# Mixers' tiles in pairs of 8 KB, the normed rows in two tiles of 16 KB, and experts' weights loaded in packets of 8 and 16 KB

## The chip, the cores and the metric

The kernel runs on one core of a Trainium2 chip. The metric is the device time of one execution in microseconds; the time of the kernel before is the median of three runs, 1653.99 us (1653.51 to 1654.05). The profile was taken from one execution of it. PE is TensorE, DVE VectorE, ACT ScalarE, POOL GpSimd and SP SyncE. SP computes nothing here: it issues nearly all of the loads.

## What the kernel computes

The reference is an encoder trunk of two layers on 512 rows of 1024 (float32). What matters of it is this:

```
for l in range(DEPTH):                       # 2
    hn = rmsnorm(x, norm_mix_w[l])
    proj = hn @ w_in[l]                      # the four mixers' columns
    mix = concat([hyena, mamba2, attention, hgrn2])
    x = x + mix @ w_out[l]
    x = x + expert_choice_moe(rmsnorm(x, norm_ffn_w[l]), router_w[l], moe_w_gate[l], moe_w_up[l], moe_w_down[l])
return rmsnorm(x, final_norm_w)

def expert_choice_moe(x, w_router, w_gate, w_up, w_down):   # 16 experts, 64 rows each
    gate, idx = top_k(softmax(x @ w_router), cap)
    xe = x[idx]
    hdn = silu(xe @ w_gate) * (xe @ w_up)    # 1024 x 1024 each
    ye = (hdn @ w_down) * gate
    return rows of ye added at idx
```

Each expert has three matrices of 4 MB, so a layer's experts have 192 MB (201 million bytes) of weights, and each is used once.

## The kernel before

A layer has two stages. In the first, the rows of x are normed and turned (`norm_T`, tiles `hT`), multiplied with the columns of `w_in`, and worked on by four mixers, whose instructions are woven together by a planner. In the second, the router's ranks pick 64 rows for each expert, and the experts follow one another on PE in the order in which they are written: up(e), the turned rows of a later expert, gate(e+1), the hidden columns, down(e); after every second expert `combine` adds the weighted rows to x (`eoT`, `eot` and `ec`: a matmul that turns the pair's ranks, a comparison on DVE, and the matmuls that place the rows).

Weights come in by `pieces` (L1371 to L1398). A matrix of an expert is 8 rows of 512 KB, each 128 partitions x 4 KB; in main memory four rows of one partition lie side by side, so that a DMA of n rows moves n x 4 KB in one run per partition. A piece goes into a slot of a pool, whose tag is taken from the list `ring`. The pools are shared with the mixers: before, H has 12 slots of 4 KB (4 hold x, 8 the turned normed rows, of which weights use 7), N 9 and B 13 of 4 KB, W 2 of 8 KB and S 3 of 8.25 KB. A slot of W or S takes two rows by one DMA, unless k is 3 or 7; then the second half is kept in `spare` and is the next row's. All else takes one row. A tile can go to a slot when the last reader of the tile that had it is done, and for a tile that was loaded in two DMAs that is the reader of its later half.

All of these DMAs stand in one queue, SP's. Its order is fixed when the program is built, by a scheduler that follows the order of the text except where it expects a slot to come free late; then it may put a DMA behind others. At run time SP takes them one after the other: one that waits holds all behind it. Eight semaphores (DMAHW0 to DMAHW7 below) are shared by them in turn. The order of PE, DVE and ACT is fixed in the same way.

The names below: `we` is a tile of weights, `eg`, `eu` and `ey` are the sums of gate, up and down, `exT` and `ehT` their turned inputs, `eh` the hidden rows, `eY` the weighted rows. The number behind a name is that of the tile.

Of the kernel before, what the change touches and what calls it, by code (L numbers as in the profile page):

```python
# [11 lines left out]
F32R = mybir.dt.float32r  # L12
# [82 lines left out]
NN, NB, NW, NS, NG, NEP, NPA = 9, 13, 2, 3, 9, 2, 3  # L95
# [15 lines left out]
def encoder(ctx: ExitStack, tc: tile.TileContext, d, out, dbg=None, stages=None, nlayers=NL):  # L111
# [6 lines left out]
    slots = {"H": (12, 4096), "N": (NN, 4096), "B": (NB, 4096), "W": (NW, 8192), "S": (NS, 8448),  # L118
             "G": (NG, 2048), "E": (NEP, 2048)}
# [82 lines left out]
    X = [tl("H", [D], "x") for _ in range(4)]  # L202
# [124 lines left out]
    def norm_T(l, rows, side=iter(())):  # L327

        hl = [[tl("H", [2, L], "hT", F32R) for _ in range(4)] for _ in range(2)]

        def scaled(q):
            xs = [tl("B", [D], "xn") for _ in range(2)]
# [16 lines left out]
        def turned(q, xs):  # L349
            for k in range(8):  # L350
# [7 lines left out]
                h, o = (hl[i][k // 2][:, k % 2, q * 256:(q + 1) * 256] for i in range(2))  # L358
# [14 lines left out]
        return ([hl[0][k // 2][:, k % 2] for k in range(8)], [hl[1][k // 2][:, k % 2] for k in range(8)])  # L373
# [79 lines left out]
    def mix_tile(m):  # L453
        MIX[m] = (tl("B", [2, L], "mxh", F32R), tl("B", [2, L], "mxl", F32R))
# [25 lines left out]
    def filter_consts():  # L480
        dec = tl("B", [4, 256], "dec")
        SY.dma_start(dec, d["c_decay"].rearrange("(t p) c -> p t c", p=P))
        kt = [tl("B", [4, 256], "kt") for _ in range(2)]
        for i in range(2):
            SY.dma_start(kt[i], d["c_kdft"][i].rearrange("(t p) f -> p t f", p=P))
        return dec, kt
# [48 lines left out]
    def filter_spec(spec, h, w3, fb, dec, kt, scratch=None):  # L535

        ab = [tl("B", [2, 2, 256], "fab") for _ in range(2)]
# [43 lines left out]
    def hyena_proj(l, hT, cols, st):  # L581
        raw1 = w_raw(l, HY0 + 256, 256)
        raw2 = w_raw(l, HY0 + 512, 256)
        uT = tl("N", [4, 256], "uT")
# [16 lines left out]
        x0 = tl("N", [2, L], "hx0")  # L601
# [8 lines left out]
    def hyena(l, st, spec):  # L610
        uT, x0 = st
        ct, it = tl("B", [2, 4, P], "dft"), tl("B", [2, 4, P], "idft")
# [3 lines left out]
        xs = [tl("B", [2, 2, 256], "hX") for _ in range(2)]  # L616
# [35 lines left out]
        zs = [tl("B", [2, 2, 256], "hz") for _ in range(2)]  # L652
# [990 lines left out]
```

## Time and profile before

| | |
|---|---|
| median of 3 runs | 1653.99 us (1653.51 to 1654.05) |
| profiled execution | 1657.14 us, span 1655.4 us |
| mean granted TensorE clock | 0.971 |
| PE busy | 1531.7 us, 93% of the span |
| DVE, ACT, POOL busy | 802.6, 396.1, 213.8 us |
| moved by DMA | 468.54 MB, 283 GB/s over the span |
| chain that ended last | PE 63%, DMA 25%, DVE 6% |
| experts' matmuls, gate, up, down (L1404) | 230.7, 237.9, 233.1 us |
| experts' DMAs of 512 KB, and of 1024 KB | 632, and 68 |

The span is what the profiler saw from the first to the last instruction. Busy time is the share in which an engine worked at all; the chain is followed back from the last instruction, at each step to what released it.

### The profile page before, as it was taken

What the parts mean: (1) busy time and instruction counts of PE and PEld (TensorE: products, weight loads), DVE (VectorE), ACT (ScalarE), POOL (GpSimd) and SP (SyncE); (2) the same over time, 40 slices, a digit from 0 to 9 for tenths busy, and PEclk for the clock granted to TensorE, in tenths of its full rate; (3) what the DMA queues carried; (4) which work ended last, traced back from release to release, by engine and by line L of the source; (5) the groups of instructions that cost most, each with busy time, mean ns of one, the idle gap of its engine ahead of it and who ended that gap; (6) DMA issues with size and microseconds to landing.
All of it is one profiled execution on the core that took longest, in us unless ns stands there. A gap on an engine that the chain in (4) does not pass through costs nothing.

```text
span 1655.4 us, 22757 instructions
## 1 busy us (share of the span) xinstructions
PE 1531.7 (93%) x8899; PEld 880.2 (53%) x8899; DVE 802.6 (48%) x1727; ACT 396.1 (24%) x805; POOL 213.8 (13%) x214
## 2 busy tenths in 40 slices
PE   6989998989999998989979999999899999998985
PEld 5778787763433432334368788787434433332332
DVE  6777677573333331432256767856533333332323
ACT  4344333431000000001162435243200001000012
POOL 3232133000000000000033232310000000000001
PEclk9989899999999999999989889999899999999998
DMA  5411223679999999999932202167799999999996
GB/s 169 127 51 36 68 77 141 239 288 341 421 420 421 421 420 399 421 420 420 419 95 82 72 27 77 54 233 266 262 407 418 420 422 420 421 420 421 420 420 247
DMA packets 153773, 468.54 MB, mean 283 GB/s; under 512 B 20440, under 2 KB 56696, under 8 KB 144962
## 3 DMA queue, kind: packets, MB, share of 16 engines
q1 hardware_dynamic: 145030, 455.10, 70.3%
q0 software_dynamic: 2240, 7.34, 1.1%
q10 hardware_dynamic: 6396, 4.65, 0.8%
q8 instruction: 70, 1.15, 0.3%
q14 instruction: 37, 0.30, 0.0%
HBM read 460.60 MB, written 6.44 MB: 282 GB/s over the span
## 4 chain that ended last, share of the span: by engine, by line
PE 63%; DMA 25%; DVE 6%; ACT 3%; issue 2%; POOL 1%; ACTq 0%; SPq 0%; DVEq 0%; POOLq 0%
PE eg L1404 9%; DMA we<-in_moe_w_up_dram 9%; DMA we<-in_moe_w_down_dram 9%; PE eu L1404 8%; PE ey L1404 7%; DMA we<-in_moe_w_gate_dram 5%; PE pcm L395 3%; PE pcm L396 3%; PE pcm L397 3%; PE ec L1475 2%; PE po L1222 2%; PE po L1223 2%; PE po L1224 2%; PE ptm L418 2%; PE ptm L417 2%
## 5 line engine op out<-in xcount | busy, mean ns | idle before, releaser
L1404 PE MATMUL eu<-we,exT 128*64 128x512 f32 x1024 | 237.9, 598 | 17.2 <-DMA we<-in_moe_w_up_dram 14.9
L1404 PE MATMUL ey<-we,ehT 128*64 128x512 f32 x1024 | 233.1, 600 | 17.3 <-ACT ehT L1440 11.2
L1404 PE MATMUL eg<-we,exT 128*64 128x512 f32 x1024 | 230.7, 598 | 10.4 <-DMA we<-in_moe_w_gate_dram 6.4
L1404 PEld LDWEIGHTS eu<-we,exT 128*64 128x64 f32 x1024 | 67.7, 136 | 181.6 <-issue 91.9
L1303 DVE SCALAR_TENSOR_TENSOR ra<-er,ra,tie 128x512 bf16<-128x512 f32 x128 | 95.9, 749 | 128.6 <-PE er L1311 125.7
L1404 PEld LDWEIGHTS ey<-we,ehT 128*64 128x64 f32 x1024 | 70.2, 137 | 155.5 <-issue 102.1
L1404 PEld LDWEIGHTS eg<-we,exT 128*64 128x64 f32 x1024 | 69.2, 136 | 149.6 <-issue 111.5
L1457 DVE SCALAR_TENSOR_TENSOR eY<-ey,erg,eY 64x512 fp32r<-64x512 f32 x64 | 48.0, 750 | 189.2 <-ACT eY L1456 189.1
L1425 ACT ACTIVATE eh<-eg 128x512 f32<-128x512 f32 x32 | 19.1, 598 | 498.6 <-PE eg L1404 498.6
L397 PE MATMUL pcm<-hT,whl 128*128 128x512 f32 x320 | 128.9, 403 | 3.5 <-DVE whl L381 3.5
L1476 DVE TENSOR_TENSOR x<-x,ec 128x512 f32<-128x512 f32 x128 | 81.0, 691 | 102.6 <-PE ec L1475 102.5
L396 PE MATMUL pcm<-hT,whl 128*128 128x512 f32 x320 | 130.2, 407 | 0.0
L395 PE MATMUL pcm<-hT,whl 128*128 128x512 f32 x320 | 129.9, 406 | 0.0
L1348 POOL DMA_INDIRECT exe<-xd,erow x28 | 27.8, 994 | 787.0 <-DVE erg L1329 660.1
L1456 ACT ACTIVATE eY<-ey,erg 64x512 fp32r<-64x512 f32 x64 | 43.7, 683 | 268.3 <-PE ey L1404 243.9
L1432 DVE TENSOR_TENSOR eh<-eh,eu 128x512 f32<-128x512 f32 x32 | 22.0, 687 | 153.9 <-PE eu L1404 153.9
L417 PE MATMUL ptm<-wtm,hT 128*128 128x256 f32 (+1 forms) x256 | 76.1, 298 | 1.7 <-DVE aqs L926 1.7
L1475 PE MATMUL ec<-eY,eot 128*128 128x512 f32 x256 | 67.3, 405 | 10.2 <-DVE erow L1346 6.4
L418 PE MATMUL ptm<-wtm,hT 128*128 128x256 f32 (+1 forms) x256 | 74.2, 291 | 1.3 <-DVE wtm L381 1.3
L380 POOL TENSOR_SCALAR whl<-wraw 128x1024 fp32r<-128x1024 f32 x40 | 46.9, 1173 | 220.1 <-PE pcm L397 127.7
L419 PE MATMUL ptm<-wtm,hT 128*128 128x256 f32 (+1 forms) x256 | 72.8, 288 | 0.0
L397 PEld LDWEIGHTS pcm<-hT,whl 128*128 128x128 f32 x320 | 62.3, 195 | 18.2 <-DVE whl L381 3.9
(394 smaller groups left out, 2374.8 us busy)
## 6 DMA issues: line engine op xcount, KB each, us to landing
we<-in_moe_w_gate_dram SPq DMA_DIRECT2D x218, 512.0 KB
we<-in_moe_w_up_dram SPq DMA_DIRECT2D x208, 512.0 KB
we<-in_moe_w_down_dram SPq DMA_DIRECT2D x206, 512.0 KB
wraw<-in_w_in_dram SPq DMA_DIRECT2D x27, 1024.0 KB
we<-in_moe_w_down_dram SPq DMA_DIRECT2D x25, 1024.0 KB
we<-in_moe_w_up_dram SPq DMA_DIRECT2D x24, 1024.0 KB
we<-in_moe_w_gate_dram SPq DMA_DIRECT2D x19, 1024.0 KB
wo<-in_w_out_dram SPq DMA_DIRECT2D x8, 1024.0 KB
```

The costliest lines, as they stand in the source:

```text
L380: G.tensor_scalar(dst_hi, raw, 1.0, 0.0, op0=ALU.mult, op1=ALU.add)
L395: T.matmul(ps, w[:, 0, k, :], H[k], start=(k == 0), stop=False)
L396: T.matmul(ps, w[:, 0, k, :], Lo[k], start=False, stop=False)
L397: T.matmul(ps, w[:, 1, k, :], H[k], start=False, stop=(k == 7))
L417: T.matmul(dst, h, w[:, 0, k % 4], start=(k == 0), stop=False)
L418: T.matmul(dst, h, w[:, 1, k % 4], start=False, stop=False)
L419: T.matmul(dst, g, w[:, 0, k % 4], start=False, stop=(k == 7))
L1303: V.scalar_tensor_tensor(g, pr, ra[:, c, e, 0:1], tie[:, 384 - c * P:896 - c * P], op0=ALU.subtract, op1=ALU.is_gt, accum_out=k)
L1404: T.matmul(ps[f][64 * f:64 * f + 64], xT[:, j, h], qs[4 * h + j][:, f * 512:(f + 1) * 512], start=(h == 0 and j == 0), stop=(h == 1 and j ...
L1457: V.scalar_tensor_tensor(lo, src, w[c, 0:1], hi.bitcast(F32), op0=ALU.mult, op1=ALU.subtract)
L1475: T.matmul(ps, ot[:, t * P:(t + 1) * P], Y[i][q][n], start=(q == 0), stop=(q == 1))
L1476: V.tensor_add(xrow(t)[:, c], xrow(t)[:, c], ps)
```

## The change

The pools are cut anew, with the same bytes in all. x has a pool of its own (X, 4 x 4 KB). The turned normed rows lie in two tiles of 16 KB (H). N has 4 and B 6 slots of 8 KB; V and C are single slots of 4 KB. The mixers' tiles that had one slot of 4 KB each are put together in twos into one tile of 8 KB and used as its halves (`MIX`, `xn`, `kt`, `fab`, `hX`, `hz`, `gqk`, `gU` with `gw`, and so on); what is left single goes to V (`gv`, `av`, `ra`) and to C (`oh`, `dec`, `mpack`). In `pieces`, a DMA takes as many rows as the tile has and as are left of the four that lie side by side. What a tile has over is kept in `spare`, and is used only for a place where the number of rows left has the same parity; so a rest can stay until a later matrix. A layer's 384 rows are then 190 DMAs in layer 0 and 193 in layer 1 where they were 351 and 349: 14 and 20 of one row, 167 and 164 of two, 9 of four. The matmuls and the engines' operations are the same in number.

```diff
-NN, NB, NW, NS, NG, NEP, NPA = 9, 13, 2, 3, 9, 2, 3
+NN, NB, NW, NS, NG, NEP, NPA = 4, 6, 2, 3, 9, 2, 3
...
-    slots = {"H": (12, 4096), "N": (NN, 4096), "B": (NB, 4096), "W": (NW, 8192), "S": (NS, 8448),
-             "G": (NG, 2048), "E": (NEP, 2048)}
+    slots = {"X": (4, 4096), "H": (2, 16384), "N": (NN, 8192), "V": (1, 4096), "B": (NB, 8192), "C": (1, 4096),
+             "W": (NW, 8192), "S": (NS, 8448), "G": (NG, 2048), "E": (NEP, 2048)}
...
-        hl = [[tl("H", [2, L], "hT", F32R) for _ in range(4)] for _ in range(2)]
+        hl = [tl("H", [8, L], "hT", F32R) for _ in range(2)]
...
-            xs = [tl("B", [D], "xn") for _ in range(2)]
+            xp = tl("B", [2, D], "xn")
+            xs = [xp[:, i] for i in range(2)]
...
-        MIX[m] = (tl("B", [2, L], "mxh", F32R), tl("B", [2, L], "mxl", F32R))
+        hl = tl("B", [2, 2, L], "mix", F32R)
+        MIX[m] = hl[:, 0], hl[:, 1]
...
-        dec = tl("B", [4, 256], "dec")
+        dec = tl("C", [4, 256], "dec")
...
-        pack = tl("B", [576], "mpack")
+        pack = tl("C", [576], "mpack")
...
-        v = tl("N", [4, 256], "av")
+        v = tl("V", [4, 256], "av")
...
-        v = tl("N", [4, 256], "gv")
+        v = tl("V", [4, 256], "gv")
...
-            qk, qi, bes = yield from hgrn_decay(l, i, q, f, lb, keep)
-            R = [tl("B", [64, 16], "gR") for _ in range(2)]
+            qi = qis[:, i]
+            qk, bes = yield from hgrn_decay(l, i, q, f, lb, keep, qi)
+            R = tl("B", [2, 64, 16], "gR")
+            R = [R[:, e] for e in range(2)]
...
-        rt = tl("H", [D], "ra")
+        rt = tl("V", [D], "ra")
...
-    FIRST = ["N"] * 2 + ["B"]
-    EARLY = ["N"] * 3 + ["B"] * 6 + ["N"] * (NN - 5) + ["B"] * (NB - 7)
+    FIRST = ["N", "C"]
+    EARLY = ["N"] + ["B"] * 3 + ["N"] * (NN - 2) + ["B"] * (NB - 3)
     LATE = ["W"] * NW + ["S"] * NS
     ring = []
 
+
     SIDE_AT = 9
-    RESTED = (["N"] * 2 + ["B"] * 6 + ["N"] * (NN - 4) + ["H"] * 7 + LATE) * 6
+    RESTED = (["N"] + ["B"] * (NB - 3) + ["N"] * (NN - 2) + ["H"] * 2 + LATE) * 6
 
     def pieces(l, view):
 
@@ -1379,20 +1396,20 @@
             rows = d["moe_w_" + m][l, e].rearrange("(h p j) f -> h p j f", h=2, p=P)
             v = view[e, m] = []
             while len(v) < 8:
+
                 k = len(v)
-                n = 1
-                if spare:
-                    t = spare.pop()
+                left = 4 - k % 4
+                t = next((t for t in spare if t.shape[1] % 2 == left % 2), None)
+                if t is not None:
+                    spare.remove(t)
                 else:
                     if not ring:
-                        ring.extend(FIRST + EARLY + ["H"] * 7 + LATE)
+                        ring.extend(FIRST + EARLY + ["H"] * 2 + LATE)
                     tag = ring.pop(0)
                     t = tl(tag, [slots[tag][1] // 4096, D], "we")
-                    if t.shape[1] == 2:
-                        if k % 4 != 3:
-                            n = 2
-                        else:
-                            spare.append(t[:, 1:])
+                n = min(t.shape[1], left)
+                if n < t.shape[1]:
+                    spare.append(t[:, n:])
                 SY.dma_start(t[:, :n], rows[k // 4][:, k % 4:k % 4 + n, :])
...
-        ring[:] = LATE + FIRST + ["H"] * 7 + EARLY + LATE
+        ring[:] = LATE + FIRST + ["H"] * 2 + EARLY + LATE
...
-        ring[:] = FIRST + ["H"] * 7 + EARLY
+        ring[:] = FIRST + ["H"] * 2 + EARLY
```

The places of the order that the prediction speaks of follow. First SP in layer 0, before: gate(2), eight rows, then the first of down(1).

```order
L1396 DMA we_3709<-in_moe_w_gate_dram 128x1024 [waits DMAHW0_49,PE_49]
L1396 DMA we_3711<-in_moe_w_gate_dram 128x1024 [waits DMAHW1_49,PE_49]
L1396 DMA we_3713<-in_moe_w_gate_dram 128x1024 [waits DMAHW2_49,PE_49]
L1396 DMA we_3715<-in_moe_w_gate_dram 128x1024 [waits DMAHW3_49,PE_49]
L1396 DMA we_3717<-in_moe_w_gate_dram 128x1024 [waits DMAHW4_49,PE_49]
L1396 DMA we_3719<-in_moe_w_gate_dram 128x1024 [waits DMAHW5_49,PE_49]
L1396 DMA we_3721<-in_moe_w_gate_dram 128x1024 [waits DMAHW6_49,PE_49]
L1396 DMA we_3723<-in_moe_w_gate_dram 128x1024 [waits DMAHW7_49,PE_49]
L1396 DMA we_3756<-in_moe_w_down_dram 128x1024 [waits DMAHW0_49,PE_49]
```

Each is one row and waits for the DMA eight before it and for an old reader of its slot. Then, further on in before, SP from gate(3)'s third DMA to up(3)'s first.

```order
L1396 DMA we_3890<-in_moe_w_gate_dram 128x1024 [waits DMAHW2_49,PE_49]
L1396 DMA we_3892<-in_moe_w_gate_dram 128x1024 [waits DMAHW3_49,PE_49]
L1396 DMA we_3894<-in_moe_w_gate_dram 128x2048 [waits DMAHW4_49,PE_49]
L1396 DMA we_3896<-in_moe_w_gate_dram 128x2048 [waits DMAHW5_49,PE_49]
L1396 DMA we_3945<-in_moe_w_down_dram 128x2048 [waits DMAHW6_49,PE_49]
L1396 DMA we_3947<-in_moe_w_down_dram 128x2048 [waits DMAHW7_49,PE_49]
L1396 DMA we_3949<-in_moe_w_down_dram 128x2048 [waits DMAHW0_49,PE_49]
L1396 DMA we_3951<-in_moe_w_down_dram 128x1024 [waits DMAHW1_49,PE_49]
L1396 DMA we_3953<-in_moe_w_down_dram 128x1024 [waits DMAHW2_49,PE_49]
L1396 DMA we_3989<-in_moe_w_up_dram 128x1024 [waits DMAHW3_49,PE_49]
```

The first of up(3) has the semaphore DMAHW3, which was last that of we_3892, the fourth row of gate(3). In after, SP has the rows of the H tile we_3128 near the start: a row of gate(0), one of up(1), and two of gate(2).

```order
L1413 DMA we_3128<-in_moe_w_gate_dram 128x1024 [waits DMAHW0_49,PE_49]
L1225 DMA wo_3039<-in_w_out_dram 128x2x1024 [waits DMAHW1_49,DVE_49]
L1413 DMA we_3130<-in_moe_w_gate_dram 128x4096 [waits DMAHW2_49,PE_49]
L1413 DMA we_3128<-in_moe_w_up_dram 128x1024 [waits DMAHW3_49]
L1413 DMA we_3128<-in_moe_w_gate_dram 128x2048 [waits DMAHW4_49]
```

And later in layer 0 of after, behind up(2) and gate(3), the last two rows of gate(2) and the first two of down(1), in the tile that takes the slot of we_3128.

```order
L1413 DMA we_3796<-in_moe_w_gate_dram 128x2048 [waits DMAHW2_49,PE_49]
L1413 DMA we_3798<-in_moe_w_gate_dram 128x2048 [waits DMAHW3_49,PE_49]
L1413 DMA we_3800<-in_moe_w_gate_dram 128x2048 [waits DMAHW4_49,PE_49]
L1413 DMA we_3802<-in_moe_w_gate_dram 128x2048 [waits DMAHW5_49,PE_49]
L1413 DMA we_3650<-in_moe_w_gate_dram 128x2048 [waits DMAHW6_49,PE_49]
L1413 DMA we_3650<-in_moe_w_down_dram 128x2048 [waits DMAHW7_49]
L1413 DMA we_3851<-in_moe_w_down_dram 128x2048 [waits DMAHW0_49]
```

The last DMAs of gate(2) have moved from their place ahead of down(1) to one behind gate(3), and wait for PE, whose matmuls of gate(2) must have read we_3128. The next is SP in after at gate(5)'s last two rows and gate(6)'s first pair.

```order
L1413 DMA we_4100<-in_moe_w_gate_dram 128x1024 [waits DMAHW0_49,PE_49]
L1413 DMA we_3897<-in_moe_w_gate_dram 128x1024 [waits DMAHW1_49]
L1413 DMA we_4150<-in_moe_w_down_dram 128x2048 [waits DMAHW2_49,PE_49]
L1413 DMA we_4152<-in_moe_w_down_dram 128x2048 [waits DMAHW3_49,PE_49]
L1413 DMA we_4154<-in_moe_w_down_dram 128x2048 [waits DMAHW4_49,PE_49]
L1413 DMA we_4156<-in_moe_w_down_dram 128x2048 [waits DMAHW5_49,PE_49]
L1413 DMA we_4192<-in_moe_w_up_dram 128x2048 [waits DMAHW6_49]
L1413 DMA we_4194<-in_moe_w_up_dram 128x2048 [waits DMAHW7_49]
L1413 DMA we_4196<-in_moe_w_up_dram 128x2048 [waits DMAHW0_49,PE_49]
L1413 DMA we_4198<-in_moe_w_up_dram 128x2048 [waits DMAHW1_49,PE_49]
L1413 DMA we_4240<-in_moe_w_gate_dram 128x2048 [waits DMAHW2_49,PE_49]
```

The tile we_3897 got its second row from gate(5) here, and we_4240 takes its slot, nine issues and 17 rows further on. Last is PE at the end of layer 1, before: the last down with `eoT` between its matmuls.

```order
L1465 MATMUL eoT_11843<-pk,erk_11272 64x128
L1404 MATMUL ey_11809<-we_11815,ehT_11807 64x512
L1404 MATMUL ey_11810<-we_11815,ehT_11807 64x512
L1465 MATMUL eoT_11843<-pk,erk_11272 64x128 x6
L1404 MATMUL ey_11809<-we_11817,ehT_11807 64x512
L1404 MATMUL ey_11810<-we_11817,ehT_11807 64x512
L1465 MATMUL eoT_11843<-pk,erk_11272 64x128
L1404 MATMUL ey_11809<-we_11819,ehT_11807 64x512
L1404 MATMUL ey_11810<-we_11819,ehT_11807 64x512
L1404 MATMUL ey_11809<-we_11819,ehT_11807 64x512
L1404 MATMUL ey_11810<-we_11819,ehT_11807 64x512
L1404 MATMUL ey_11809<-we_11821,ehT_11807 64x512
```

And the same place in after.

```order
L1421 MATMUL ey_11104<-we_11108,ehT_11102 64x512
L1421 MATMUL ey_11105<-we_11108,ehT_11102 64x512
L1421 MATMUL ey_11104<-we_11108,ehT_11102 64x512
L1421 MATMUL ey_11105<-we_11108,ehT_11102 64x512
L1421 MATMUL ey_11104<-we_11110,ehT_11102 64x512
L1421 MATMUL ey_11105<-we_11110,ehT_11102 64x512
L1421 MATMUL ey_11104<-we_11110,ehT_11102 64x512
L1421 MATMUL ey_11105<-we_11110,ehT_11102 64x512
L1482 MATMUL eoT_11132<-pk,erk_10634 64x128 x8
L1492 MATMUL ec_11145<-eY_11065,eot_11141 128x512
L1492 MATMUL ec_11145<-eY_11067,eot_11141 128x512
L1492 MATMUL ec_11149<-eY_11066,eot_11141 128x512
```

The matmuls of `eoT` have moved from between those of the last down to behind them.

## Rows read from the trace of the kernel before

**Rows 1.** The page: busy time of PE, and the chain by engine.

```profile
PE 1531.7 (93%) x8899; PEld 880.2 (53%) x8899; DVE 802.6 (48%) x1727; ACT 396.1 (24%) x805; POOL 213.8 (13%) x214
...
PE 63%; DMA 25%; DVE 6%; ACT 3%; issue 2%; POOL 1%; ACTq 0%; SPq 0%; DVEq 0%; POOLq 0%
```

**Rows 2.** Table by stage; columns in its first line.

```profile
core 0: us, PE busy (x) PEld busy (x) DVE busy (x) ACT busy (x) POOL busy (x), PEclk, DMA share, GB/s
...
120.00:180.00 60.00, 58.87 (x549) 48.92 (x549) 42.10 (x72) 21.71 (x36) 11.60 (x13) 0.83 0.12 36
...
360.00:390.00 30.00, 24.92 (x132) 8.87 (x134) 15.23 (x58) 5.00 (x12) 0.00 (x0) 0.89 0.67 239
...
480.00:600.00 120.00, 116.78 (x622) 46.38 (x618) 42.38 (x102) 11.61 (x18) 6.72 (x8) 1.00 1.02 420
...
1200.00:1300.00 100.00, 97.69 (x528) 38.56 (x525) 33.06 (x87) 9.56 (x15) 6.74 (x8) 1.00 1.02 414
```

**Rows 3.** Chain of waits, experts of layer 0, then 1: start us, us, what.

```profile
373.92 7.08 PE eg L1404 x32
...
417.84 7.09 PE eg L1404 x32
...
426.35 7.09 PE ey L1404 x32
...
440.99 1.05 PE eoT L1465 x16
...
479.21 7.09 PE ey L1404 x32
...
497.90 7.02 PE eg L1404 x32
...
576.23 11.73 DMA we<-in_moe_w_down_dram
...
828.28 3.39 PE ey L1404 x15
...
1365.37 10.54 DMA we<-in_moe_w_up_dram
```

**Rows 4.** What SP waited for, experts of layer 0: us, times, longest.

```profile
SPq L1396 <- DMA we<-in_moe_w_up_dram: 102.0, 101, 2.7
...
SPq L1396 <- PE eu L1404: 11.9, 22, 4.7
```

**Rows 5.** The page: DMAs of two rows, those of down.

```profile
we<-in_moe_w_down_dram SPq DMA_DIRECT2D x25, 1024.0 KB
```

**Rows 6.** Table by stage: a stretch of pairs, then one of single rows.

```profile
617.00:627.00 10.00, 9.37 (x42) 2.55 (x38) 3.59 (x10) 1.37 (x2) 0.00 (x0) 1.00 1.02 427
...
481.00:513.00 32.00, 31.22 (x174) 13.65 (x172) 14.07 (x35) 2.56 (x4) 1.68 (x2) 1.00 1.03 420
```

**Rows 7.** DMA packets in 520 to 528 us, and below in 532 to 562.

```profile
DMA packets 470, 3.42 MB, mean 428 GB/s; under 512 B 52, under 2 KB 52, under 8 KB 52
...
DMA packets 3459, 12.58 MB, mean 419 GB/s; under 512 B 392, under 2 KB 392, under 8 KB 3458
```

**Rows 8.** Timeline of SP: start us, us over all issues, how many.

```profile
419.82 11.42 SPq L1396 DMA_DIRECT2D we<-in_moe_w_up_dram  x5
...
497.24 9.69 SPq L1396 DMA_DIRECT2D we<-in_moe_w_gate_dram  x8
```

**Rows 9.** Chain of waits near 55 us: small DMAs, issue to landing.

```profile
55.42 2.45 DMA mbc<-in_m_D_dram
...
60.51 2.14 DMA mbc<-in_m_D_dram
```

**Rows 10.** End of layer 1: chain, then timeline of PE, then of DVE.

```profile
1635.14 1.99 PE ey L1404 x8
...
1637.84 0.50 PE L1475 MATMUL ec<-eY,eot 128*128 128x512 f32 x1 [0.77 <-ACT eY L1456]
...
1633.21 0.75 DVE L1468 TENSOR_SCALAR eot<-eoT,pk 128x512 fp32r<-128x512 f32 x1 [6.11 <-PE eoT L1465]
1637.82 1.53 DVE L1457 SCALAR_TENSOR_TENSOR eY<-ey,erg,eY 64x512 fp32r<-64x512 f32 x2 [3.87 <-ACT eY L1456]
```

More of the change, by code (lines that the diff above doesn't have):

```diff
@@ L200, in w_in_rows @@
         return d["w_in"][l][:, c0:c0 + n].rearrange("(k p) c -> p k c", p=P)
-    X = [tl("H", [D], "x") for _ in range(4)]
+    X = [tl("X", [D], "x") for _ in range(4)]
     xr = d["x"].rearrange("b (t p) d -> p (b t) d", p=P)
@@ L357, in turned @@
                 w = nmix[:, l, k:k + 1]
-                h, o = (hl[i][k // 2][:, k % 2, q * 256:(q + 1) * 256] for i in range(2))
+                h, o = (hl[i][:, k, q * 256:(q + 1) * 256] for i in range(2))
                 A.activation(h, src, AF.Copy, scale=w)
@@ L372, in norm_T @@
         turned(1, ys)
-        return ([hl[0][k // 2][:, k % 2] for k in range(8)], [hl[1][k // 2][:, k % 2] for k in range(8)])
+        return [[h[:, k] for k in range(8)] for h in hl]
     def split(raw, dst_hi, dst_lo, pool=False):
@@ L535, in filter_spec @@
     def filter_spec(spec, h, w3, fb, dec, kt, scratch=None):
-        ab = [tl("B", [2, 2, 256], "fab") for _ in range(2)]
+        ab = tl("B", [2, 2, 2, 256], "fab")
+        ab = [ab[:, i] for i in range(2)]
         for t in range(4):
@@ L611, in hyena @@
         uT, x0 = st
-        ct, it = tl("B", [2, 4, P], "dft"), tl("B", [2, 4, P], "idft")
+        both = tl("B", [2, 2, 4, P], "dft")
+        ct, it = both[:, 0], both[:, 1]
         SY.dma_start(ct, d["c_dft"].rearrange("i c t f -> t i c f"))
         SY.dma_start(it, d["c_idft"].rearrange("i c f t -> f i c t"))
-        xs = [tl("B", [2, 2, 256], "hX") for _ in range(2)]
+        xs = tl("B", [2, 2, 2, 256], "hX")
+        xs = [xs[:, i] for i in range(2)]
         (x0_, x1), (x2, x3) = ([x[:, i] for i in range(2)] for x in xs)
@@ L650, in hyena @@
             yield 3
-        zs = [tl("B", [2, 2, 256], "hz") for _ in range(2)]
+        zs = tl("B", [2, 2, 2, 256], "hz")
+        zs = [zs[:, i] for i in range(2)]
         z = [zs[0][:, 0], zs[1][:, 0], zs[0][:, 1], zs[1][:, 1]]
@@ L829, in mamba @@
         yield 2
-        y = tl("B", [4, 256], "my")
         def rows(t):
@@ L933, in attn_proj @@
             ps = proj_cm(hT, raw, i * P, AM[1])
-            kh, kl = (tl("N", [2, L], "aks", F32R) for _ in range(2))
+            both = tl("N", [2, 2, L], "aks", F32R)
+            kh, kl = both[:, 0], both[:, 1]
             for h in range(2):
@@ L961, in logits @@
             if b == 0 and h == 0:
-                tab[i] = [tl("B", [896], "atab") for _ in range(2)]
+                two = tl("B", [2, D], "atab")
+                tab[i] = [two[:, g, :896] for g in range(2)]
                 for g in range(2):
@@ L1036, in hgrn_proj @@
         yield from pv
-        f = []
+        f = tl("N", [2, 2, L], "gf")
+        f = [f[:, e] for e in range(2)]
         for e in range(2):
```

67 lines of the change are left out of this document (37 added, 30 removed).

## The prediction

> **What bounds the kernel now.** I read the page first, then the table by stage, then the chain of waits in the expert stages, and last what SP waits for.
>
> The page calls it a TensorE kernel: PE is busy 93% of the span and holds 63% of the chain, DMA 25% [rows 1]. That is an average over stages with different limits. In the table by stage the DMA engines are at 0.12 in the emptiest stage of the mixers and at 1.02, that is full, in the experts' stages (480 to 600 us in layer 0, 1200 to 1300 in layer 1); there they move 420 and 414 GB/s [rows 2]. The chain says when this decides. Up to 576.23 us it runs from matmul to matmul and experts come every 26.4 us (the downs at 426.35 and 479.21 are two experts apart) [rows 3]. A row of weights is 512 KB, 524,288 bytes, which at 420 GB/s takes 1.248 us; an expert has 24 rows, 30.0 us. So the stream is 3.5 us per expert slower than PE, eats its head start, and from 576.23 us (1365.37 us in layer 1) the chain is mostly DMA [rows 3]. What SP waits for agrees: 102.0 us for landings of the ups' weights, the largest of three such sums, against 11.9 us for PE to read a slot, the largest of its three [rows 4]. SP's DMAs share eight semaphores in turn, so each stands until the one eight before it has landed: at most eight are under way. If PE alone set the pace, down(15) would start seven pairs of experts, 370 us, after down(1) at 426.35 us and end 7.1 us later, near 803.5 us. The chain has it end at 831.7 us [rows 3]. So some 28 us of this layer are there for a faster stream to win, and a gap in the stream is not made up by PE: it moves the end.
>
> **The gain: rate.** Before, 68 DMAs in both layers are of two rows (25 of down [rows 5], 24 of up, 19 of gate), 136 of 768 rows; after, of 384 rows about 14 to 20 come alone, 36 in DMAs of four, the rest in pairs. Before has two stretches of some 10 us in which it is pairs that land, at 427 [rows 6] and 428 GB/s [rows 7], against 420 and 419 in stretches of 32 and 30 us of single rows [rows 6, 7]. In packets: of the 470 of the one pair stretch 52 are under 8 KB, of the 3459 of the other kind all but one [rows 7]. A row at 427 takes 1.228 us, 0.020 less; by the extremes (428 against 419 [rows 7]) 0.026 less. Some 29 rows of a layer, counted in program order, are loaded before its experts start and cost nothing, so 2 x 355 rows lie in the stream. 82% of a layer's rows came alone and 4% do now, so 78% change from 4 KB to more: 555 rows. 555 x 0.0225 = 12.5 us. Bounds: 555 x 0.020 = 11.1, and 555 x 0.026 = 14.4 plus a second step of that size for the 72 rows in packets of 16 KB, about 16. Before has no weights in packets of 16 KB; from below, they could be no better than 4 KB (-1.5 us). I take no gain from 8 to 16 KB.
>
> The rule that speaks against the size of this gain is in the Trainium skill, "DMA: Bandwidth & Descriptors", "Why small descriptors are slow": a packet carries a fixed overhead of about three cycles beside its 32-byte beats. As an estimate from that page of the Trainium skill, 131 cycles for 128 beats against 259 for 256 make 1.2%, 8 us in place of 12.5, and the sum would be 1662 us. The trace has 1.7 to 1.9%, and I go by the trace.
>
> **Cost 1: a wait inside SP's queue, once per layer.** In before SP asks for gate(2) right after up(1), each row in a slot that is long free. In after the DMA of gate(2)'s rows 6 and 7 (the tile we_3650, 16 KB a partition) has moved behind up(2) and gate(3): its slot is the one whose rests were given to up(1) and to rows 0 and 1 of gate(2), so it waits until PE has read these. All 72 rows up to gate(3), less those two and the two of down(1) that share the tile, 68, stand ahead of it. In before the 68th row is gate(3)'s fourth; up(3)'s first DMA, eight behind it on the same semaphore, is issued at 419.82 us [rows 8], so the 68th row has landed by then. The release: gate(2) starts at 417.84 us and takes 7.09 us for 8 rows [rows 3], so two rows are read at 419.6 us. A small DMA takes 2.14 to 2.45 us from issue to landing [rows 9], so nothing arrives until about 421.9 us, 2 us after the queue has run dry. SP stands at it from about 402 us (14 rows, 17.5 us, are under way when it gets there), so nothing behind it can fill the gap. Cover: if the start is late by 1 to 2 us, the 68 rows land that much later and the gap shrinks to nothing. If PE comes late to gate(2), having waited for a pair in up(0), down(0) or up(1), the gap grows by as much; each of those stages now waits for 1 MB, 2.5 us, where 512 KB, 1.25 us, did. Bounds 0 and 6 per layer, I take 4: 8 us for both. The rows that PE itself needs (gate(2)'s row 6, due at 423.1 us) come near 424.5: 1.4 us of PE's slack.
>
> **Cost 2: a shorter one of the same kind.** The DMA of gate(6)'s first pair takes the slot whose second half went to gate(5)'s last row, only 17 rows ahead of it in the queue. gate(5) ends at 497.90 + 7.02 = 504.9 us [rows 3]. In before SP issues gate(6)'s rows from 497.24 us on [rows 8] without such a wait; with about 10 us from issue to landing, the queue would be dry at about 507 to 508.5 us, and a DMA released at 504.9 lands from 507.2 on. Bounds 0 and 4 per layer, I take 1.5, near the lower because that row shows just enough cover: 3 us.
>
> **Cost 3: the start.** While the first matrices run, slots come free one row at a time as PE reads them, and the rate is only 239 GB/s in 360 to 390 us [rows 2]. A pair is free only when its second row is read, 7.09 / 8 = 0.89 us later [rows 3], and a tile of four 2.7 us later. Bounds 0 and 2.7, I take 1.5 per layer: 3 us.
>
> **Cost 4: the ends.** The last rows of both layers come in pairs and fours, so PE starts each later; the last DMA of before is a pair too (8 matmuls after it, 1.99 us [rows 10]), so only the tiles ahead of it count: 0 to 2 us, I take 1. In layer 1 the matmuls that turn the last pair's ranks (eoT) stood between those of the last down; now they stand behind all of them. Before, the eot is made at 1633.21 us, before the last weights start PE again at 1635.14 us, and the first ec starts 0.71 us after the last ey [rows 10]. Now eoT (1.05 us for 16 [rows 3]) starts after ey and is done before DVE has made the two eY (1.53 us from 0.69 us after ey); eot (0.75 us) stands behind these on DVE: ec starts 0.69 + 1.53 + 0.75 = 2.97 us after ey instead of 0.71. The second ec needed the second eY of ACT, at 1.42 us, so 1.6 us of it are new. Bounds 0 and 2.3.
>
> **The mixers.** The operations are the same; two tiles in one slot mean that a new pair waits for the later of the two old readers, and the three tiles in the one slot V (gv, av, ra) and the three in C follow one another. PE is busy 58.9 of 60 us in 120 to 180 [rows 2], DMA at 0.12: nothing there is near a limit, and SP has the time. I take 0, bounds -1 and +5 (one row of two raw projections late, 2 x 2.5 us, in one layer).
>
> **Sum.** -12.5 + 8 + 3 + 3 + 1 + 1.6 = +4.1 us. The profiled execution took 1657.14 us, 3.1 above the median of 1653.99, so it would be 1661.2; on the median's footing 1658.1.
>
> **Rivals.**
> *The queue covers the waits (faster).* Eight DMAs of 1 MB are 20 us of work where eight of 512 KB are 10. If the gaps at gate(2) close (the stream starting 1 to 2 us late is enough) and the start costs nothing more, only the ends are left: -12.5 + 1 + 1.6 + 2 to 3 = -8, 1646; with half of cost 1, -4, 1650. For it: that the two-row stretches show their rate with SP waiting as always. Against it: the slot's release at 419.6 us is PE's, and no queue depth helps when every row ahead has landed by 419.8. It decides from a gap below 1.5 us per layer.
> *Balance.* Gap 1 is 2 us as the bare arithmetic gives: the sum is 0, 1654, between 1651 and 1657.
> *The rate does not come.* The 427 GB/s belong to short bursts, and a steady stream of pairs is held to 420 by something else. Then the gain is 0 and the costs stand: 1654 + 16.6 = 1670; with half of the gain, 1664. Against it: both stretches show the same rate with no idle time ahead of them.
> *The mixers wait.* A pair that waits for the later reader on the path: +5 on top, 1663. Against it: row 120 to 180 above.
>
> **How the numbers follow.** Forecast with costs as taken 0.42 (own range 1655 to 1662), covered 0.20, balance 0.15, no rate 0.13, mixers 0.10. About 0.2% (3.3 us) is what a measurement can tell from no change. Faster by more: most of the covered case and a little of balance, 0.21. Within: a quarter of the forecast, most of balance, a little of the covered case, 0.25. Slower: 0.54. The range reaches to the covered case's 1646 and to 1668, between half and all of the missing rate.
>
> **What would show it.** DMA rate in 480 to 600 us at 427 or above (rate right) or at 420 (wrong). SP waiting on PE's gate matmul for about 15 us near 403 to 420 us and near 1215 to 1232, and in the DMA rate a dip of 2 to 6 us right after it; no dip means that cost 1 is wrong. A second dip near 507. Between the last ey and the first ec about 3 us. The gate of expert 0 starting within 1 us of before's 373.92 us (mixers right). The prediction is wrong if the stages from 396 to 830 us shrink by more than 3 us.

## The result, and the profile after

The changed kernel takes 1672.93 us in the median of 4 runs (1671.46 to 1675.05), the kernel before, on the same chip, 1654.02 (1653.51 to 1658.03): an estimated ratio of 1.0098 with a 95% interval of [1.0069, 1.0126] (the plain quotient of these two medians is 1.0114). It is slower by 1%, where 0.25% was forecast, and lies above the forecast's upper end of 1668. The times of before spread with the clock that the execution was granted (1649.95 to 1664.57 us in a later group of 31 runs, from a mean of 0.974 down to 0.966), so each ratio below is to the runs of before on the same chip at the same time, and is an estimate of the same kind.

The profiled executions show where it went. Each row runs from one landmark of the chain to the next (first gate of expert 0, last down of expert 15):

| us | before | after | difference |
|---|---|---|---|
| mixers of layer 0, to gate(0) | 373.92 | 385.43 | +11.5 |
| experts of layer 0 | 457.8 | 459.5 | +1.7 |
| mixers of layer 1 | 354.5 | 353.5 | -1.0 |
| experts of layer 1 | 451.0 | 452.8 | +1.8 |
| from there to the end | 18.3 | 20.8 | +2.5 |
| span | 1655.4 | 1672.0 | +16.6 |

(The differences are rounded each, so that they add up to 16.5.) So most of the loss stands where the prediction had put nothing: in layer 0's mixers. The page of after, the lines that answer to [rows 1, 5]:

```profile
PE 1535.8 (92%) x8899; PEld 892.5 (53%) x8899; DVE 804.5 (48%) x1727; ACT 395.6 (24%) x805; POOL 211.1 (13%) x214
...
PE 61%; DMA 25%; DVE 7%; ACT 3%; issue 2%; POOL 0%; ACTq 0%; SPq 0%; DVEq 0%; POOLq 0%
...
we<-in_moe_w_gate_dram SPq DMA_DIRECT2D x113, 1024.0 KB
```

PE does the same 8899 instructions in 4 us more. The shares hardly tell the two kernels apart, since an average over stages hides both what was won and what was lost. Next is the table by stage of after, the columns of [rows 2].

```profile
60.00:80.00 20.00, 16.80 (x38) 9.13 (x37) 13.10 (x37) 9.31 (x18) 3.20 (x4) 0.67 0.28 45
...
120.00:180.00 60.00, 55.27 (x508) 47.56 (x508) 43.45 (x67) 30.89 (x45) 13.37 (x16) 0.80 0.12 35
...
360.00:390.00 30.00, 24.61 (x155) 15.04 (x155) 19.02 (x75) 10.10 (x32) 0.00 (x0) 0.89 0.54 201
...
420.00:480.00 60.00, 56.79 (x306) 22.96 (x304) 20.60 (x47) 6.49 (x10) 3.36 (x4) 1.00 0.97 402
...
480.00:600.00 120.00, 116.85 (x642) 48.24 (x640) 41.42 (x99) 11.44 (x18) 8.40 (x10) 1.00 1.01 421
...
540.00:590.00 50.00, 48.73 (x268) 20.27 (x264) 18.94 (x44) 5.12 (x8) 2.38 (x3) 1.00 1.01 427
```

In 540 to 590 us SP waits for landings alone and for no slot, and the stream runs at 427 GB/s, which the prediction had asked for; 402 and 421 in the wider stretches are the same rate with gaps in it. The row to look at is the first. In 60 to 80 us PE did 38 instructions, at a granted clock of 0.67 (1.00 is 2.4 GHz, 0.50 would be 1.2 GHz throughout). The same stretch of before:

```profile
60.00:80.00 20.00, 19.31 (x90) 14.81 (x89) 16.74 (x43) 12.13 (x23) 5.02 (x7) 1.00 0.36 69
```

There it did 90 at 1.00. PE's timeline shows what happened. First before, then after: start, us, instruction, and in brackets the idle time before it with its releaser.

```profile
66.08 3.70 PE L540 MATMUL f<-fw,fy 64*128 64x512 f32 x8 [0.69 <-ACT fy L478]
```

```profile
66.92 3.78 PE L543 MATMUL f<-fw,fy 64*128 64x512 f32 x4 [3.20 <-ACT fy L480]
...
71.77 3.78 PE L543 MATMUL f<-fw,fy 64*128 64x512 f32 x4
```

`f` are the matmuls of the filter's last layer, and `fy`, made on ACT, is the sine that they read. PE stood 3.20 us for it where it had stood 0.69, and then four matmuls took what eight had taken. The chain of after (start, us, what) says how long that lasted:

```profile
70.69 0.72 PE pcm L397
...
80.12 0.43 PE pcm L397
80.54 0.30 PE pcm L398
80.84 0.24 PE pcm L396
...
83.60 3.45 PE fk L564 x16
...
385.43 7.08 PE eg L1421 x32
```

A `pcm` (projection) follows the last by 0.43 us until 80.5 and by 0.23 from then on; in before it was 0.23 all along but for the first, and `fk`, the filter's next matmuls, started at 73.64. Of the 9.96 us between the two `fk`, 2.5 are the longer wait (3.20 - 0.69), 3.8 the slow `f` (7.49 on the chain against 3.70), and 3.0 the slow `pcm` (9.20 us for the 26 behind `f`, less 16 that took 3.85 in before and ten more at 0.23). The last 0.6 is the rest of PE's work ahead of `f`. So 10 of the 11.5 us are there by `fk`; where the other 1.5 arise was not followed.

Why PE waited has two parts. In program order `f` stands behind 118 `pcm` and no longer behind 128, so PE reached it at 63.72 us (66.92 - 3.20) where it had at 65.39. And the sine came 0.8 us later. SP's queue and ACT's, before:

```profile
41.65 0.57 SPq L482 DMA_DIRECT2D dec<-in_c_decay_dram  x1
...
59.37 0.61 ACTq L190 DMA_DIRECT2D mbc<-in_m_dt_bias_dram  x1
...
65.40 0.63 ACT L478 ACTIVATE fy<-fy 128x512 f32<-128x512 f32 x1
```

And after:

```profile
51.85 0.37 SPq L484 DMA_DIRECT2D dec<-in_c_decay_dram  x1
56.85 0.37 SPq L386 DMA_DIRECT2D wraw<-in_w_in_dram  x1
...
58.09 2.57 ACTq L190 DMA_DIRECT2D mbc<-in_m_dt_bias_dram  x1
...
66.23 0.63 ACT L480 ACTIVATE fy<-fy 128x512 f32<-128x512 f32 x1
```

`dec` now shares the one slot of C with `oh` and is loaded ten microseconds later; the raw weights behind it in SP's queue go out at 56.85 us, and a small load on ACT's queue takes 2.57 us to issue, not 0.61. The sine is behind it on ACT. What holds that load is in no row (a semaphore shared with SP is a guess); that it goes back to `dec`'s place is shown below, by a run in which `dec` is elsewhere.

In the experts' stages the holes are where they were forecast. What SP waited for in layer 0 (us, times, longest; 7.1 us in all of this kind before) and the timeline of its queue:

```profile
SPq L1413 <- PE eg L1421: 65.8, 12, 19.5
...
412.61 19.05 SPq L1413 DMA_DIRECT2D we<-in_moe_w_gate_dram  x5
```

And what the DMA engines moved, in slices of 1 us from 420 us on:

```profile
GB/s 426 410 434 434 426 434 418 434 344 98 41 33 229 369 418 426 418 426 418 442 442 401 434 426 442 401 451 393 422 438 434 397 447 418 442 426 434 410 451 410
```

From 428 to 434 us six slices together lack 1448 GB/s against 427 each: 3.4 us of transfer lost. The chain names it, and below it the timeline of PE. PE reads the first two rows of gate(2), which releases the held DMA; this takes 5.25 us to land; PE reads the four rows behind meanwhile and then stands 1.90 us for the held ones.

```profile
429.35 1.96 PE eg L1421 x8
431.33 5.25 DMA we<-in_moe_w_gate_dram
...
436.62 1.94 PE L1421 MATMUL eg<-we,exT 128*64 128x512 f32 x8 [1.90 <-DMA we<-in_moe_w_gate_dram]
```

The same hole of layer 1 costs 3.0 us. At the end of layer 1, chain of after, to [rows 10]:

```profile
1644.07 7.14 PE ey L1421 x32
1651.21 0.67 ACT eY L1473
1651.90 0.76 DVE eY L1474
1652.68 0.76 DVE eY L1474
1653.47 0.76 DVE eot L1485
1654.37 3.55 PE ec L1492 x8
```

From the end of `ey` to the first `ec` it is 3.16 us, where 2.97 was worked out. The `ec` themselves are slow here. PE's timeline, first of after, then of a version in which one number of the planner's differs (the first under "The place of `f`", below):

```profile
1654.37 5.37 PE L1492 MATMUL ec<-eY,eot 128*128 128x512 f32 x16 [2.33 <-DVE eot L1485]
...
1646.19 3.87 PE L1492 MATMUL ec<-eY,eot 128*128 128x512 f32 x16 [2.33 <-DVE eot L1485]
```

The wait is the same; the granted clock is 0.72 in 1654.4 to 1660 us of after and 1.00 in 1646.2 to 1650.2 us of the other, whose end takes 19.9 us and not 20.8.

### The profile page after: what moved, and what is told of

The parts are those of the page before. It is cut to its first block, busy times and chain, and to the rows that moved or that the text cites. A ratio compares the mean times of both kernels' runs of the same rounds, so it can differ in the third digit from the quotient of the medians.

```text
span 1672.0 us, 22058 instructions
## 1 busy us (share of the span) xinstructions
PE 1535.8 (92%) x8899; PEld 892.5 (53%) x8899; DVE 804.5 (48%) x1727; ACT 395.6 (24%) x805; POOL 211.1 (13%) x214
## 4 chain that ended last, share of the span: by engine, by line
PE 61%; DMA 25%; DVE 7%; ACT 3%; issue 2%; POOL 0%; ACTq 0%; SPq 0%; DVEq 0%; POOLq 0%
DMA we<-in_moe_w_up_dram 9%; DMA we<-in_moe_w_gate_dram 9%; PE eg L1421 8%; PE ey L1421 8%; PE eu L1421 8%; DMA we<-in_moe_w_down_dram 6%; PE pcm L396 3%; PE pcm L397 3%; PE pcm L398 3%; PE ec L1492 2%; PE po L1238 2%; PE po L1239 2%; PE po L1240 2%; PE ptm L419 2%; PE ptm L418 2%
## 5 line engine op out<-in xcount | busy, mean ns | idle before, releaser
L1421 PE MATMUL eu<-we,exT 128*64 128x512 f32 x1024 | 233.9, 599 | 16.2 <-DMA we<-in_moe_w_up_dram 15.9
L1421 PEld LDWEIGHTS eu<-we,exT 128*64 128x64 f32 x1024 | 71.5, 137 | 172.9 <-issue 125.1
L398 PE MATMUL pcm<-hT,whl 128*128 128x512 f32 x320 | 131.5, 411 | 6.1 <-DVE whl L382 6.1
L396 PE MATMUL pcm<-hT,whl 128*128 128x512 f32 x320 | 132.3, 414 | 0.0
L397 PE MATMUL pcm<-hT,whl 128*128 128x512 f32 x320 | 131.6, 411 | 0.0
L1492 PE MATMUL ec<-eY,eot 128*128 128x512 f32 x256 | 68.4, 411 | 11.5 <-DVE erow L1362 6.4
```

What stands on the lines that cost most here:

```text
L396: T.matmul(ps, w[:, 0, k, :], H[k], start=(k == 0), stop=False)
L397: T.matmul(ps, w[:, 0, k, :], Lo[k], start=False, stop=False)
L398: T.matmul(ps, w[:, 1, k, :], H[k], start=False, stop=(k == 7))
L1421: T.matmul(ps[f][64 * f:64 * f + 64], xT[:, j, h], qs[4 * h + j][:, f * 512:(f + 1) * 512], start=(h == 0 and j == 0), stop=(h == 1 and j ...
L1492: T.matmul(ps, ot[:, t * P:(t + 1) * P], Y[i][q][n], start=(q == 0), stop=(q == 1))
```

## The experiments

Theory A: the 11.5 us come of PE's wait at `f`, through the clock; the experts' stages lose to the held tiles and gain from the rate, as forecast. Rivals: B, the mixers lose time at many places, from the paired slots as such; C, larger packets bring no rate in this kernel, and the experts' +1.7 us are small costs without a gain. Gate(0)'s start, and the experts' time as in the table above, are read in the profiled execution of each.

**Packets alone.** Same order and same slots, but each DMA of n rows split into n.

```diff
-                SY.dma_start(t[:, :n], rows[k // 4][:, k % 4:k % 4 + n, :])
+                for i in range(n):
+                    SY.dma_start(t[:, i:i + 1], rows[k // 4][:, k % 4 + i:k % 4 + i + 1, :])
```

> The changed kernel with every DMA of n rows of weights issued as n DMAs of one row each, so that all packets are of 4 KB; tiles, slots and the order of the rest stay. Theory A (larger packets bring the stream from 420 to 427 GB/s, worth 12 us): the rate in undisturbed stretches falls to 419 to 421 and the time rises by 9 to 14 us, to 1682 to 1687. Rival (the higher rate is that of fewer, deeper queued DMAs or costs nothing): same within 4 us.

1681.31 us, 1.016 [1.012, 1.0199]. The undisturbed stretch, same columns as above:

```profile
540.00:590.00 50.00, 48.69 (x268) 20.33 (x266) 19.12 (x45) 5.12 (x8) 2.37 (x3) 1.00 1.03 419
```

419 against 427 GB/s: the packets alone make 1.9%, and C falls. The time rose by 8.4 us in the medians, just short of the 9 to 14 expected. The experts take 463.0 and 456.6 us, 3.5 and 3.9 more than after. That is less than the 6.2 us per layer of the prediction's rate; part of it is that the second dip, 1.4 us in after, is missing here (419 GB/s in 505 to 535 us, the full rate of this kernel, where after has 405); the rest of the difference is not accounted for. Gate(0) starts at 385.4 as in after, so the loss of the mixers has nothing to do with packets.

**Without rests.** A tile goes only where all of it is used at once, so that no slot waits for a later matrix.

```diff
-                t = next((t for t in spare if t.shape[1] % 2 == left % 2), None)
...
+                tag = ring.pop(next((i for i, g in enumerate(ring) if slots[g][1] // 4096 <= left), 0))
```

> The changed kernel with no rests of tiles: a tile of 16 KB is taken only where four rows are left, the single slot C takes no weights, so every DMA has 2 or 4 rows and no slot waits for a rest. Theory A (the two dips per layer, 3.4 and 1.4 us, are SP standing at a slot whose rest was given to a later matrix): both dips go and the time falls by 6 to 10 us, to 1663 to 1667. Rival (the dips are PE being late, or the smaller buffer of one row less brings them back elsewhere): dips of the same sum stay, and the time is 1670 or more. The filter's place in the mixers is not touched, so the gate of expert 0 still starts near 385 us by both.

1659.4 us, 1.0025 [1.0007, 1.0043]. The experts take 453.6 and 447.3 us, 5.9 and 5.4 less than after and 4.2 and 3.7 less than before. The stretch with the hole:

```profile
420.00:480.00 60.00, 58.47 (x328) 24.22 (x326) 21.42 (x50) 5.44 (x9) 3.37 (x4) 1.00 1.01 427
```

It is 427 where after has 402. So the holds cost 5.4 to 5.9 us per layer. The DMA rows show 3.4 (3.0 in layer 1) at the first and, as dips of some 1.4 us near 518 and 1333, the second; the last 1 us is not accounted for, and the edit also takes away the DMAs of one row. Gate(0) still starts at 382.5, and PE still waits 3.19 us at `f`: the mixers' loss is another matter. The time is below the expected 1663 to 1667 because two more things changed: the scheduler put `eoT` between the last `ey` again, which took the end from 20.8 to 18.6 us, and the fall of the clock behind `f` was shorter (0.74 in 60 to 80 us, where after has 0.67).

**The place of `f`.** One number of the planner's table puts `f` behind 130 `pcm`; in a second version another puts it behind 144.

```diff
-FW = (3, 5, 5)
+FW = (3, 5, 9)
```

```diff
-FW = (3, 5, 5)
+FW = (4, 5, 5)
```

> The changed kernel with one number changed: the planner's step after the filter's second layer costs 9 instead of 5, so that 130 instead of 118 projection matmuls stand ahead of the filter's first matmul f in PE's order. Theory A (one idle stretch of PE of 3.2 us before f at 63.7 us drops the granted clock for 13.7 us, and that is most of what layer 0's mixers lost): the wait before f falls below 1 us, the clock stays at its upper level there, the gate of expert 0 starts at 375 to 378 us instead of 385.4, and the time is 1662 to 1666 us. Theory B (pairs of tiles wait for the later of two readers all over the mixers, f is only one place): the gate starts at 383 us or later and the time is 1669 us or more.

> The changed kernel with the planner's first number 4 instead of 3: one more step of the projection is written ahead of the filter, and f stands behind 144 instead of 118 projection matmuls, some 6 us later. Theory A (the clock falls because PE waits 3.2 us before f): no wait before f, no fall of the clock between 60 and 100 us, gate of expert 0 at 374 to 377 us, time 1661 to 1665. Theory B (paired tiles wait all over the mixers): gate at 383 or later, 1669 or more.

1666.4 us, 1.0058 [1.0033, 1.0083], and 1666.29 us, 1.0049 [1.0032, 1.0065]. Gate(0) starts at 376.8 and 375.7, some 9 us of the 11.5 back. Not all of it is the edit's: the run with `eoT` moved (below), whose edit leaves the mixers alone, has its gate(0) at 382.6 with 3.30 us of wait, so some 3 us lie between one execution and another. By the medians and by the ratios the two are 6.5 to 8 us faster than after. The first of them at `f`:

```profile
67.27 2.61 PE L543 MATMUL f<-fw,fy 64*128 64x512 f32 x4 [1.71 <-ACT fy L480]
```

The wait is halved (1.71 us, in the second 1.75), and 60 to 80 us has a granted clock of 0.83 and 0.88 in place of 0.67. B falls: every slot is paired as in after. The wait is not gone, and neither is all of the fall; both versions had been expected to have less than 1 us of wait, and both times lie above their expected ranges.

The control is the kernel before with the second of these numbers.

> The kernel before with the planner's first number 4 instead of 3, as a control. Before has only 0.7 us of wait at f and no fall of the clock there, so theory A expects no gain from more matmuls ahead of f: 1652 to 1658 us. If it falls by more than 4 us, the edit is good by itself and what it gave the changed kernel says less about the cause.

1659.22 us, 1.0006 [0.9982, 1.0031]: no gain. There PE does not wait at `f`, but elsewhere, at `tbp` for `oh`:

```profile
59.29 3.49 PE L909 MATMUL tbp<-oh,rb 33*4 33x512 f32 x4 [2.95 <-DMA oh<-in_c_bucket_dram]
...
60.00:66.00 6.00, 6.00 (x11) 1.70 (x10) 2.61 (x4) 0.00 (x0) 0.00 (x0) 0.50 0.22 73
```

The four matmuls take 3.49 us where before's take 1.88, and gate(0) starts at 380.3. So the clock falls behind a wait in a kernel without paired tiles too, which speaks against B once more. The number helps after because of the wait that after has, not in itself.

**`dec` out of the slot of `oh`.** The same kernel was profiled twice.

```diff
-        dec = tl("C", [4, 256], "dec")
+        dec = tl("B", [2, 4, 256], "dec")[:, 0]
```

> The changed kernel with the decay table dec in a slot of B (8 KB, half of it unused) instead of the single slot C, which it shares with the table oh of the attention. Theory C (the wait of PE before f comes from that sharing: SP's load of dec stands until oh has been read, at 51.85 us, and the raw projection weights behind it land late and hold the semaphore that ACT's small loads need next): dec is loaded before 30 us, ACT's load of mbc does not take 2.6 us any more, the wait before f falls below 1.5 us, the gate of expert 0 starts at 374 to 378 us, and the time is 1661 to 1666. Rival (the wait is there because the program order puts f 10 matmuls too early whatever dec does; here it stands 6 too early): wait 2 us or more, gate after 381, time 1668 or more.

> The kernel with dec in a slot of B once more, for one more profile: its ten times lay in two groups, near 1661 and near 1669 us, and the profile taken is of the first. Theory A says that the two differ in whether the clock falls after PE's wait before f: a profile of the second group has f's matmuls at twice their time and the gate of expert 0 8 us later than 372.6; one of the first group looks as before. By the rival the two differ elsewhere, with the same start of the gate.

1668.15 us in the median, 1.0047 [1.0024, 1.0071], in two groups: four of ten runs from 1661.07 to 1665.4, six from 1668.04 to 1670.84; a further execution took 1672.38. The loads are released: `dec` goes out at 19.47 us, the load on ACT's queue issues in 0.65 us again, and the sine starts at 64.48 us, 0.9 before that of before. The wait expected below 1.5 us is 1.73, though, and the median misses the expected 1661 to 1666: what is left of the wait is the part of the order, since PE, with six `pcm` fewer ahead of `f` than in before, is there at 63.43 us. PE's timeline and stage row in the first profile, and gate(0) on the chain:

```profile
65.16 3.71 PE L543 MATMUL f<-fw,fy 64*128 64x512 f32 x8 [1.73 <-ACT fy L480]
...
60.00:80.00 20.00, 18.27 (x84) 13.85 (x83) 15.66 (x41) 14.32 (x27) 5.90 (x7) 1.00 0.31 73
...
372.65 7.08 PE eg L1421 x32
```

And in the second, the same program:

```profile
65.63 6.72 PE L543 MATMUL f<-fw,fy 64*128 64x512 f32 x8 [1.93 <-ACT fy L480]
...
60.00:80.00 20.00, 18.07 (x51) 11.24 (x50) 12.47 (x37) 11.81 (x23) 4.14 (x4) 0.74 0.31 71
...
381.10 7.09 PE eg L1421 x32
```

The wait differs by 0.2 us, gate(0) by 8.45, and the program is the same: behind the wait the clock fell in one execution and not in the other. 5.4 of the 8.45 us are there by `fk` (74.10 and 79.50 us on the chains); the other 3.0 come later, where the second profile has a granted clock of 0.93 from 120 us to gate(0) and the first 0.95. In the first, gate(0) comes 1.3 us earlier than in before, so in this execution, in which the clock stays up, pairing the slots costs the mixers nothing. Over the executions profiled, 0.69 us of wait at `f` (before) was followed by no fall; 1.73 by none, and 1.71, 1.75 and 1.93 by one (0.83, 0.88 and 0.74 in 60 to 80 us); 3.05 to 4.27 by a fall in all of seven (0.67 to 0.83). At the last `ec` the wait of 2.33 us of after came in six executions, and a fall behind it in two.

**No wait at all?** The constants' loads put ahead together, and their exponential behind them, should bring the sine forward; once in after, once without rests and with `eoT` moved (below).

```diff
         return bc
+
+    def mamba_decay(bc):
...
+            for m in range(NL):
+                mamba_decay(mbc[m])
```

> The changed kernel with dec in a slot of B, and with the small loads of both layers' constants issued together by ACT, the two Exp behind all of them, so that ACT waits once instead of twice for a small DMA ahead of the filter's sine. Theory A: fy is ready 3 to 4 us sooner, PE does not wait at f, the clock does not fall between 60 and 100 us in any execution, the gate of expert 0 starts at 371 to 376 us, and the time is 1656 to 1662 us. Theory B (the mixers lose by paired tiles): gate after 381, 1669 or more.

> The last one's edits on the version without rests of tiles and with eoT ahead of the last down. If they add up: gate at 371 to 376 us, experts' stages 453 and 447 us, 1643 to 1650 us, 0.5 to 0.8% faster than the kernel before. If the mixers meet a fall of the clock elsewhere: 1651 to 1656.

1675.67 us, 1.0116 [1.0094, 1.0138], and 1667.26, 1.0074 [1.0056, 1.0092]: the intervention failed. The sine then stood behind a product on DVE (ACT idle for 5.80 us until it), and PE waited longer:

```profile
69.08 7.19 PE L543 MATMUL f<-fw,fy 64*128 64x512 f32 x8 [4.27 <-ACT fy L480]
```

So neither shows this place without a wait. Both ran slow behind it (60 to 80 us at 0.74 and 0.68), which A asks for, and no more can be read from them on the mixers. In the second the experts of layer 0 take 457.6 us, only 0.1 less than in before, and those of layer 1 446.5: from 600 to 845 us its stream moves 406 to 412 GB/s, where the first version without rests has 419 and 427 in 600 to 800. Why was not followed.

**`eoT` ahead of the last down.** It is written before the last `ey`.

```diff
+            if e == NE - 1:
+                rows = combine(e // 2)
+                next(rows)
```

> The changed kernel with eoT of the last pair written ahead of the last down; one look at the tail. From the last ey to the end of the span the changed kernel took 20.8 us and before 18.3. If eoT's place is the cause, 18.3 to 19; if the tail differs for another reason, above 20. The rest as in the changed kernel.

One execution, 1668.79 us. The end on the chain:

```profile
1640.60 1.02 PE eoT L1482 x16
1641.62 6.92 PE ey L1421 x32
...
1649.22 0.69 ACT eY L1473
```

From the last `ey` to the end it is 18.5 us, where after has 20.8 and before 18.3. That is not 2.3 us for `eoT`'s place alone: in the four executions that have `eoT` behind the last `ey` as after has, but no fall of the clock at `ec` (both numbers for `f`, and `dec` moved, twice), the end takes 19.8 to 19.9 us. So its place costs 1.3 to 1.6 us, and the fall behind the wait the last 1.0 of after. In the runs with packets alone and without rests, where `eoT` stands between the `ey` again without this edit, the end takes 18.6.

**Together.** No rests, `eoT` moved, and one or the other number for `f`.

> The changed kernel with the filter step of 9, no rests of tiles, and the eight matmuls of eoT of the last pair written ahead of the last down. If all three are what they seem and add up: 1673 - 9 - 8 - 2 = 1654 us, from 1650 to 1657. If the clock falls elsewhere in the mixers instead (the rival on the mixers): 1660 or more.

> The changed kernel with the planner's first number 4, no rests of tiles (as in the run without rests) and eoT written ahead of the last down. If PE has no wait before f: gate of expert 0 at 374 to 378, experts' stages of 453 and 447 us, time 1648 to 1652, which beats the kernel before by 0.3 to 0.5%. If the clock falls at another place of the mixers instead: 1655 or more.

1655.28 us, 0.9991 [0.9974, 1.0008], and 1655.19, 0.997 [0.9951, 0.9988] (before beside it 1656.79 and 1658.31). The second beats before by 0.3% (by the medians 0.2%); the first can't be told from it. The experts take 452.8 and 446.6 us, 5.0 and 4.4 less than before. The first lies in its expected range, but by other terms: gate(0) comes 4.8 us earlier than in after, not 9, and the experts' stages are 12.8 us shorter, not 8. The gain of the earlier runs for layer 0 doesn't add up, though: gate(0) starts at 380.6 and 379.3, since PE meets another wait later on, here in the second:

```profile
127.33 0.66 PE L1189 MATMUL go<-gv,gP 128*128 128x64 f32 x2 [4.53 <-DVE gP L1186]
```

In after this wait is 0.5 us. Why the versions with both changes meet it was not settled. That second version is also the only one of the changed kernel's in which `f` comes without a wait: its eight matmuls take 3.71 us, and the granted clock is 1.00 in 66 to 80 us. It has a fall before that (0.72 in 60 to 66 us), behind 1.83 us of wait at `tbp`.

## Why the prediction was wrong

**The step that failed** is "The mixers. The operations are the same; ... nothing there is near a limit, and SP has the time. I take 0, bounds -1 and +5". It was +11.5 us in layer 0 and -1.0 in layer 1 (8.7 in layer 0 in the run with `eoT` moved, whose edit leaves the mixers alone). The argument rested on a row of 120 to 180 us; the loss is at 60 to 80, in a stretch that wasn't read. The prediction named the three tiles in C that "follow one another", and priced them at nothing: one of them, `dec`, stood in SP's queue until `oh` had been read, which sent the sine 0.8 us late. It did not look at where the scheduler now put `f` (ten `pcm` earlier, 1.7 us). Both would have been within its +5. What put them beyond is the size of the answer: behind 2.5 us of extra wait the matmuls took 6.8 us more at the lower clock, and that is a term that it did not have. Its rival "the mixers wait" had the place, 0.10, and too small a price, and the mechanism that it names, a pair that waits for its later reader, is not what the rows show.

**The rate** was right: 427 GB/s, and 419 for the same order in packets of 4 KB. By the sign that it had set, the rate in 480 to 600 us, it would count as wrong (421), but the second dip lies in that stretch. By the rule of the Trainium skill that the prediction weighed ("DMA: Bandwidth & Descriptors", "Why small descriptors are slow") the difference would have been 1.2%, an estimate; the trace has 1.9%, and the measurement decides. The whole of it does not reach the end: without the holds a layer is 4.2 and 3.7 us shorter, and the prediction's terms, per layer, for rate, start and ends sum to -6.2 + 1.5 + 0.5 = -4.2.

**Costs 1 and 2** were right in place and size. Forecast were 4 and 1.5 us per layer; the holes are 3.4 (3.0 in layer 1) and 1.4, and taking them away brings 5.9 and 5.4. SP did not stand "about 15 us" at the first but 19.05 (its own working, from 402 to 419.6 us, makes 17.6), and PE stood 1.90 us for the held rows where 1.4 was worked out. With the start and the ends, 1.3 us per layer were forecast for the experts, and 1.7 and 1.8 measured.

**The tail**: 1.6 forecast, +2.5 measured. The term was right: where the clock stays up at `ec`, the end takes 19.8 to 19.9 us, 1.5 to 1.6 more than in before. The other 1.0 is the same term that the mixers' sum lacked, a fall of the clock behind a wait (2.33 us, for `eot`).

Rivals: "the queue covers the waits" and "balance" are out by the hole of 3.4 us, "the rate does not come" by 427 against 419. Without layer 0's mixers the difference of the spans is 16.6 - 11.5 = +5.1 us, where +4.1 was forecast; 1.0 of it is that fall at the end. Whether layer 0 would be at 374 in every execution without PE's wait is argued from the execution that stayed at full clock; the two kernels without that wait (the control and the second version put together) had others.

## What to carry to other kernels

When tiles are put into other slots, read in the order of the new kernel, for every stage in which PE is the bound, which load now waits for a slot, what stands behind it on its queue, and where the scheduler has moved the matmul that depends on it. A wait of two or three microseconds ahead of a dense run of matmuls can cost several times its length (here 2.5 more of wait, 9.3 with what followed), so it is worth checking the granted clock behind each such wait before costing it at its own length. And a rest of a tile should not be kept for a later matrix, since the slot then waits for the later reader: only where every tile was used at once did larger packets make the experts' stages shorter (by 3.7 to 5.0 us each, but for one stage of one version), and the whole kernel faster (0.997) in only one of the versions, with the place of `f` and `eoT` changed too.

## What was unexpected of the hardware

The same program, with the same wait before `f` (1.73 and 1.93 us), ran on at full clock in one execution and at half in the next: eight matmuls in 3.71 and in 6.72 us, the next landmark 5.4 us and gate(0) 8.45 us apart. The two levels are in the rows: `pcm` at 0.23 us apart and at 0.43. The Trainium skill, "TensorE: Matmul & The Clock Gate" (Part 1), says that a throttled clock is the default, that activity releases it, and that the number of slow matmuls at a kernel's start changes from run to run of one kernel; the traces agree on the change from run to run, with those numbers, but here it is in the middle of a kernel. The same page of the Trainium skill puts the penalty of the slow start at under 1% of a typical kernel's span; this fall in the middle cost 8.45 of 1659.4 us, 0.5%, about twice what the forecast as a whole was about. And it is not the only place: the last `ec`, behind the same 2.33 us of wait, took 5.37 us in one execution and 3.87 in another.
